# Seven half products in place of eight in a feed-forward's first product

## The chip, the cores and the metric

The kernel runs on one core of one Trainium2 chip, as one program. The metric is the device time of one execution in microseconds (us); the times shown are medians of several runs. A core has TensorE (PE, matrix products), VectorE (DVE), ScalarE (ACT), GpSimd (POOL) and SyncE (SP, whose queue issues most DMAs). Each engine works through its own instructions in order; semaphores join them.

## The reference

What is computed is a trunk of two layers over 256 tokens of width 1024. A layer is feed-forward, attention (three kinds, merged by gates), a second feed-forward and a gated embedding. The part that the change touches:

```
def rms_norm(x, g):
    y = x * rsqrt(mean(x * x, axis=-1) + 1e-6)
    return y * g

def swiglu(x, wi, wo):                  # wi 1024 x 5632, wo 2816 x 1024
    gate, up = split(x @ wi, 2, axis=-1)
    return (silu(gate) * up) @ wo

for i in range(2):
    h = h + 0.5 * swiglu(rms_norm(h, norm_g[i, 0]), ffn1_wi[i], ffn1_wo[i])
    ...                                 # attention, added to h
    h = h + 0.5 * swiglu(rms_norm(h, norm_g[i, 2]), ffn2_wi[i], ffn2_wo[i])
    h = h + sigmoid(rms_norm(h, norm_g[i, 3]) @ w_ple_gate[i]) * (p[i] @ w_ple[i])
return rms_norm(h, final_norm)
```

## The kernel before

**Tiles.** The 256 tokens are two tiles t0 and t1 of 128. Tokens are the stationary operand of a matmul (128 x 128: 128 of the 1024 inputs by 128 tokens), weights the moving one (128 x 512). A product over 1024 inputs is eight such k blocks.

**Three matmuls per product.** Each fp32 number is split in a high part, which the matrix unit's fp32r type holds, and a low rest. `mul3` (L234 to L237) adds xh·wh, xh·wl and xl·wh into one PSUM bank. `split` makes the two parts: ACT copies the high part (L228), DVE subtracts it from the source (`sub`, L223).

**Weights.** They are streamed in pieces of 512 KB (128 x 1024 fp32, two k blocks of one 512-wide column group). `load` issues a DMA on SP into a `raw` buffer (L278; four of them), and splits it into `wh` and `wl` (six of each). `queue` lists the pieces in the order of use; `fetch` runs two pieces ahead of the product (`AHEAD`).

**A feed-forward.** `ffn` is the same for all four. Its first product has 11 column groups (`FG`), each with 256 gate and 256 up columns. `product` walks the eight k blocks of a group for both tiles, t1 some blocks behind t0 (`SKEW`): 11 x 8 x 2 x 3 = 528 matmuls into the banks `ff`. When a group is done, `gated` takes silu of the gate half on ACT (L474) and multiplies by the up half on DVE (L475). Two groups fill a 128 x 512 tile, which `turn_by_dma` transposes: DVE copies the low and high 16-bit halves apart (`cut`, L442), two DMAs on SP transpose them (`flip`, L443), and later DVE joins them (`whole`, L448), whereupon they are split into gT. The second product (`fo`) takes gT as tokens.

**Tokens.** `Norm.turn` transposes half a tile (4 x 128) on PE into a bank `nt`; `Norm.turned` scales it by the norm's gain, per 128 columns one ACT copy (L336) and one DVE subtraction (L340), into nT. The first norm takes its tokens ready transposed from memory (`xt`).

**Space and order.** The pool `blk` has six buffers of 1 MB, shared by nT, xt and the attention's tiles; `stage` has four of 128 x 512. PSUM has two banks each of `mm` and `s`, three of `tp`, one of `y`. Which instruction stands where in each engine's row is set when the program is built, by a scheduler that works from priorities (`tc.high_priority`) and the tiles' uses; buffers come free in the order of use, and the instruction that takes one waits for its last reader.

Of the kernel before, what the change touches and what calls it, by code (L numbers as in the profile page):

```python
# [10 lines left out]
F32 = mybir.dt.float32  # L11
F32R = mybir.dt.float32r
# [174 lines left out]
def trunk(ctx: ExitStack, tc: tile.TileContext, a: dict, out: bass.AP, index: list):  # L187
# [21 lines left out]
    def tp_bank(name):  # L209
        return bank("tp", 3, name)  # L210
# [8 lines left out]
    def stage(name="stage"):  # L219
        return base.tile([128, 512], F32, tag="stage", bufs=4, name=name)  # L220

    def sub(o, x, y):
        nc.vector.tensor_tensor(o, x, y, op=ALU.subtract)  # L223

    def split(hi, lo, src, scale=None):

        if scale is None:
            nc.scalar.activation(hi, src, AF.Copy)  # L228
# [5 lines left out]
    def mul3(ps, xh, xl, wh, wl, start, stop):  # L234
        nc.tensor.matmul(ps, xh, wh, start=start, stop=False)  # L235
        nc.tensor.matmul(ps, xh, wl, start=False, stop=False)  # L236
        nc.tensor.matmul(ps, xl, wh, start=False, stop=stop)  # L237

    def transposes(ps, srcs):
        w = srcs[0].shape[-1]  # L240
# [7 lines left out]
    class Weights:  # L248


        def __init__(self, width, pieces, per):
            self.width, self.per = width, per
            self.tiles = [None] * len(pieces)
            self.at = [len(queue) + j for j in range(len(pieces))]
            queue.extend((self, j, src, n) for j, (src, n) in enumerate(pieces))
# [9 lines left out]

    def fetch(n):
        while fetched[0] < min(n, len(queue)):
            w, j, src, width = queue[fetched[0]]
            w.tiles[j] = load(src, width, 2 if fetched[0] < 2 else 1)
            fetched[0] += 1  # L270

    def load(src, n, parts=1):
        raw = base.tile([128, SUB], F32, tag="raw", bufs=RAWS, name="raw")
        hi = base.tile([128, SUB], F32R, tag="wh", bufs=WBUFS, name="wh")
        lo = base.tile([128, SUB], F32R, tag="wl", bufs=WBUFS, name="wl")
        for p in range(parts):
            s = slice(p * n // parts, (p + 1) * n // parts)
            nc.sync.dma_start(raw[:, s], src[:, s])  # L278
# [7 lines left out]
        where[i, n] = (pos, c)  # L286
        pos += c

    def streamed(i, name, width):
        p, c = where[i, name]  # L290
        return Weights(width, [(a["wst"][p + j], SUB) for j in range(c)], SUB // width)

    def last_product(lhs, nk, done, name, w):

# [10 lines left out]
    def product(lhs, nk, done, name, w, skew=SKEW):  # L305

        def run():
            ps = [None] * NT
            for step in range(nk + skew):
                for t, k in ((0, step), (1, step - skew)):  # L310
                    if 0 <= k < nk:
                        wh, wl = w(k)
                        if k == 0:
                            ps[t] = product_bank(f"{name}{t}")
                        xh, xl = lhs(t, k)
                        mul3(ps[t][:, :w.width], xh, xl, wh, wl, k == 0, k == nk - 1)
                        if k == nk - 1:
                            with tc.high_priority(offset=150):
                                done(t, ps[t])
                        flow.tick()  # L320
        return run


    class Norm:
        def __init__(self, row):
            self.row = row
            self.stat = [stats[:, row, t, :] for t in range(NT)]
            self.T = [None] * NT

        def turned(self, t, k, src, pin=False):  # L330

            if self.T[t] is None:
                self.T[t] = blk("nT")
            T, n = self.T[t], src.shape[-1] // 128
            for m in range(n):
                ins = nc.scalar.activation(T[:, 0, k + m, :], src[:, 128 * m:128 * m + 128], AF.Copy, scale=ngt[:, self.row, k + m:k + m + 1])  # L336
                if pin:
                    tc.keep_in_program_order(ins)
            for m in range(n):
                nc.vector.scalar_tensor_tensor(T[:, 1, k + m, :], src[:, 128 * m:128 * m + 128], ngt[:, self.row, k + m:k + m + 1],  # L340
                                               T[:, 0, k + m, :].bitcast(F32), op0=ALU.mult, op1=ALU.subtract)

        def turn(self, t, c):
            ps = tp_bank("nt")
# [87 lines left out]
    def halves(x):  # L432

        return x.bitcast(U16).rearrange("p (n w) -> p n w", w=2)

    def turn_by_dma(pool, src, m):


        cut = stage("cut").bitcast(U16).rearrange("p (w n) -> p w n", w=2)
        flip = pool.tile([128, 2, 4, 128], U16, tag="flip", bufs=3, name="flip")  # L440
        for w in range(2):
            nc.vector.tensor_copy(cut[:, w, :128 * m], halves(src)[:, :128 * m, w])  # L442
            nc.sync.dma_start(flip[:, w, :m], cut[:, w, :128 * m], transpose=True)  # L443

        def collect():
            whole = stage("whole")
            for w in range(2):
                tc.keep_in_program_order(nc.vector.tensor_copy(  # L448
                    halves(whole)[:, :128 * m, w], flip[:, w, :m].rearrange("p a b -> p (a b)")))
            return whole[:, :128 * m].rearrange("p (k q) -> p k q", q=128)  # L450
        return collect

    def ffn(i, n, norm, after, aside=None):
        pool = None
        gT, held, pending = [None] * NT, {}, {}
# [7 lines left out]
        def collect(t):  # L463
            if t in pending:
                first, m, whole = pending.pop(t)
                split(gT[t][:, 0, first:first + m, :], gT[t][:, 1, first:first + m, :], whole())

        def gated(f):
            def done(t, ps):
                collect(t)  # L470
                if f % 2 == 0:
                    held[t] = pool.tile([128, 512], F32, tag="gated", bufs=4, name="gated")
                act = pool.tile([128, 256], F32, tag="act", bufs=3, name="act")
                nc.scalar.activation(act, ps[:, :256], AF.Silu, scale=norm.r(t))  # L474
                nc.vector.tensor_tensor(held[t][:, 256 * (f % 2):256 * (f % 2) + 256], act, ps[:, 256:], op=ALU.mult)  # L475
                if f % 2 or f == FG - 1:
                    first, m = f - f % 2, 2 * (f % 2 + 1)
                    pending[t] = 2 * first, m, turn_by_dma(pool, held[t], m)
            return done

        def gathered(t, k):
            if k == 8:
                collect(t)
            return gT[t][:, 0, k, :], gT[t][:, 1, k, :]

        steps = []

        def beside():
            if not steps:
                steps.append(aside(pool))  # L490
            next(steps[0])

        yield begin
        for f in range(FG):
            yield product(norm.lhs, NK, gated(f), "ff", streamed(i, f"{n}{f}", 512), 2 if aside and f == 0 else SKEW)
            if aside and f in (4, 5, 8):
                yield beside
# [618 lines left out]
    def setup(pool):  # L1116
# [16 lines left out]
        tb_ps = tp_bank("tb")  # L1133
        nc.tensor.matmul(tb_ps[:NB, :REV], relb, onehot, start=True, stop=True)
        tb = pool.tile([NB, REV], F32, name="tb")
# [6 lines left out]
        lprod = pool.tile([128, 4, 64], F32, name="lprod")  # L1142
# [104 lines left out]
```

## Time and profile before

| what | value |
|---|---|
| median of three runs | 1339.92 us (1339.54 to 1340.08) |
| profiled execution, span | 1338.5 us, TensorE clock 0.999 |
| PE busy | 1322.5 us (99%), 6414 matmuls |
| PE weight loads | 1091.2 us (82%), beside the matmuls |
| DVE busy | 948.1 us (71%) |
| ACT busy | 778.7 us (58%) |
| DMA | 257.14 MB, mean 192 GB/s |

The profiled execution is one run with the profiler on; its span goes from the first instruction to the last, and the runs' times also hold what lies around it. Busy shares are of the span. PE is busy in nearly all of it, and matmuls overlap one another, so that their durations add to more than their spacing. The four feed-forwards' first products stand at about 5 to 131, 461 to 581, 671 to 792 and 1120 to 1241 us of the span.

### The profile page before, as it was taken

What the parts mean: (1) busy time and instruction counts of PE and PEld (TensorE: products, weight loads), DVE (VectorE), ACT (ScalarE), POOL (GpSimd) and SP (SyncE); (2) the same over time, 40 slices, a digit from 0 to 9 for tenths busy, and PEclk for the clock granted to TensorE, in tenths of its full rate; (3) what the DMA queues carried; (4) which work ended last, traced back from release to release, by engine and by line L of the source; (5) the groups of instructions that cost most, each with busy time, mean ns of one, the idle gap of its engine ahead of it and who ended that gap; (6) DMA issues with size and microseconds to landing.
All of it is one profiled execution on the core that took longest, in us unless ns stands there. A gap on an engine that the chain in (4) does not pass through costs nothing.

```text
span 1338.5 us, 18237 instructions
## 1 busy us (share of the span) xinstructions
PE 1322.5 (99%) x6414; PEld 1091.2 (82%) x6414; DVE 948.1 (71%) x1791; ACT 778.7 (58%) x1378; POOL 18.6 (1%) x36
## 2 busy tenths in 40 slices
PE   9999999999999999999999999999999999999997
PEld 7778888888887788888888888888888878888886
DVE  6677566768978767665767765677688886767665
ACT  7555455668756655544655545566695656555454
POOL 0000000000000000000000000000000000000000
PEclk9999999999999999999999999999999999999999
DMA  8887665345652577675567875744556435877662
GB/s 298 220 260 221 210 200 202 115 159 192 221 162 90 187 206 220 209 217 180 197 191 222 216 213 188 245 152 152 180 162 220 144 101 180 238 221 214 191 208 79
DMA packets 121993, 257.14 MB, mean 192 GB/s; under 512 B 56944, under 2 KB 62500, under 8 KB 121902
## 3 DMA queue, kind: packets, MB, share of 16 engines
q1 hardware_dynamic: 121150, 254.34, 61.2%
q0 software_dynamic: 320, 1.08, 0.3%
q8 instruction: 50, 0.82, 0.3%
q10 hardware_dynamic: 432, 0.56, 0.1%
q14 instruction: 41, 0.34, 0.1%
HBM read 243.33 MB, written 1.08 MB: 183 GB/s over the span
## 4 chain that ended last, share of the span: by engine, by line
PE 91%; DMA 3%; DVE 3%; ACT 1%; issue 1%; SPq 0%; POOLq 0%; POOL 0%; DVEq 0%; ACTq 0%
PE ff L236 11%; PE ff L235 11%; PE ff L237 11%; PE fo L235 6%; PE fo L236 6%; PE fo L237 6%; PE gate L235 3%; PE gate L237 3%; PE gate L236 3%; PE s L537 2%; PE A L236 2%; PE A L235 2%; PE A L237 2%; PE br L235 2%; PE br L236 2%; PE br L237 1%
## 5 line engine op out<-in xcount | busy, mean ns | idle before, releaser
L223 DVE TENSOR_TENSOR wl<-raw,wh 128x1024 fp32r<-128x1024 f32 (+1 forms) x448 | 539.1, 1213 | 160.6 <-ACT wh L228 154.7
L228 ACT ACTIVATE wh<-raw 128x1024 fp32r<-128x1024 f32 (+1 forms) x448 | 468.0, 1051 | 228.0 <-PE fo L237 85.0
L236 PE MATMUL ff<-wl,nT 128*128 128x512 f32 x704 | 273.4, 391 | 1.8 <-DVE wl L223 1.7
L237 PE MATMUL ff<-wh,nT 128*128 128x512 f32 x704 | 272.6, 390 | 0.0
L235 PE MATMUL ff<-wh,nT 128*128 128x512 f32 x704 | 270.4, 391 | 0.5 <-ACT nT L336 0.5
L236 PEld LDWEIGHTS ff<-wl,nT 128*128 128x128 f32 x704 | 132.3, 188 | 31.2 <-DVE wl L223 4.0
L235 PEld LDWEIGHTS ff<-wh,nT 128*128 128x128 f32 x704 | 132.2, 188 | 29.8 <-ACT wh L228 1.1
L237 PEld LDWEIGHTS ff<-wh,nT 128*128 128x128 f32 x704 | 132.3, 188 | 27.4
L236 PE MATMUL fo<-wl,gT 128*128 128x512 f32 x352 | 134.2, 392 | 0.0
L237 PE MATMUL fo<-wh,gT 128*128 128x512 f32 x352 | 133.7, 389 | 0.0
L235 PE MATMUL fo<-wh,gT 128*128 128x512 f32 x352 | 132.5, 389 | 0.0
L474 ACT ACTIVATE act<-ff,stats 128x256 f32<-128x256 f32 x88 | 41.4, 471 | 85.3 <-PE ff L237 85.1
L475 DVE TENSOR_TENSOR gated<-act,ff 128x256 f32<-128x256 f32 x88 | 36.6, 417 | 65.3 <-ACT act L474 65.2
L235 PEld LDWEIGHTS fo<-wh,gT 128*128 128x128 f32 x352 | 66.1, 188 | 13.9
L237 PEld LDWEIGHTS fo<-wh,gT 128*128 128x128 f32 x352 | 66.1, 188 | 13.4
L236 PEld LDWEIGHTS fo<-wl,gT 128*128 128x128 f32 x352 | 66.1, 188 | 13.3
L235 PE MATMUL gate<-wh,nT 128*128 128x512 f32 x192 | 76.8, 400 | 0.0
L236 PE MATMUL gate<-wl,nT 128*128 128x512 f32 x192 | 76.2, 397 | 0.0
L237 PE MATMUL gate<-wh,nT 128*128 128x512 f32 x192 | 75.9, 395 | 0.0
L228 ACT ACTIVATE gT<-whole 128x512 fp32r<-128x512 f32 (+1 forms) x48 | 28.4, 591 | 64.5 <-DVE whole L448 64.3
L548 ACT ACTIVATE p<-p,st 128x128 f32<-128x128 f32 (+1 forms) x128 | 56.7, 446 | 6.3 <-DVE st L546 6.1
L448 DVE COPY whole<-flip 128x512 uint16<-128x512 uint16 (+1 forms) x96 | 38.1, 434 | 12.8 <-DMA flip<-cut 12.1
(301 smaller groups left out, 1994.5 us busy)
## 6 DMA issues: line engine op xcount, KB each, us to landing
raw<-in_wst SPq DMA_DIRECT2D x438, 512.0 KB, 4.4
band<-table SPq DMA_DIRECT2D x10, 512.0 KB, 4.7
raw<-in_wbv SPq DMA_DIRECT2D x4, 420.0 KB, 3.1
flip<-cut SPq DMA_TRANSPOSE x96, 4.0
xt<-in_xt SPq DMA_DIRECT2D x4, 256.0 KB, 5.8
raw<-in_wst SPq DMA_DIRECT2D x4, 256.0 KB, 4.5
h<-in_x SPq DMA_DIRECT2D x2, 512.0 KB, 7.8
band<-table POOLq DMA_DIRECT2D x2, 512.0 KB, 5.5
```

What stands on the lines that cost most here:

```text
L223: nc.vector.tensor_tensor(o, x, y, op=ALU.subtract)
L228: nc.scalar.activation(hi, src, AF.Copy)
L235: nc.tensor.matmul(ps, xh, wh, start=start, stop=False)
L236: nc.tensor.matmul(ps, xh, wl, start=False, stop=False)
L237: nc.tensor.matmul(ps, xl, wh, start=False, stop=stop)
L448: tc.keep_in_program_order(nc.vector.tensor_copy(halves(whole)[:, :128 * m, w], flip[:, w, :m].rearrange("p a b -> p (a b)")))
L474: nc.scalar.activation(act, ps[:, :256], AF.Silu, scale=norm.r(t))
L475: nc.vector.tensor_tensor(held[t][:, 256 * (f % 2):256 * (f % 2) + 256], act, ps[:, 256:], op=ALU.mult)
L537: nc.tensor.matmul(o, q[r, x, qb[m], t * 128:(t + 1) * 128], kk, start=x + y == 0, stop=x == 1)
L548: nc.scalar.activation(p[j], p[j], AF.Exp, bias=st[:, j:j + 1], scale=-1.0, accum_out=st[:, n + j:n + j + 1])
```

## The change

Two pairs of column groups in each feed-forward, (2, 3) and (8, 9), are computed by another formula (`Seven`, `seven`, `combine`). A pair is a product of a 2 x 2 array of token blocks (two tiles by two halves of the inputs) with a 2 x 2 array of weight blocks (two halves of the inputs by two column groups). It takes eight half products of 12 matmuls; the new code takes seven products of sums of blocks, the banks p1, p5, p6 and p7 holding them. The first product then has 504 matmuls, not 528.

- Token sums: four per feed-forward (`combine`, one DVE operation each, L565, and a split into `xs`). They need all scaled tokens kept (`xg`, in a `blk` buffer).
- Weight sums: `Seven.make` loads the blocks into x and y (two areas in `blk` buffers) and into raw buffers (L301), and subtracts them on DVE in place (`minus`, L223 with outputs x, y or raw, 128 x 1024): eight per pair. Each of the seven blocks is then split like plain weights, two pieces each.
- Results: the bank p1 is copied to v by ACT (L617), and five additions per pair on DVE join the banks.
- Order: `lines` cuts the product into 42 lines of 12 matmuls: four of the first plain group, then 14 lines of sevens mixed among 24 plain ones. Seven-lines come in the order 11, t1, t2, t3, 22, 21, t4.
- `turn_by_dma` parts the halves with one ACT operation of 1024 16-bit elements, transposes them by one DMA of eight 128-blocks, and joins them with one DVE copy. It is collected three lines later.
- `Norm.turned` scales 512 columns at once on DVE (L409), copies the high part on ACT (L410) and subtracts on DVE.
- The set-up's table product goes to an `mm` bank, and two small tiles share others' space.

```diff
+    class Seven:
...
+        order = ("11", "t1", "t2", "t3", "22", "21", "t4")
...
+        def __init__(self, i, fa, fb, x, y):
+            self.src = {"11": (fa, 0), "12": (fb, 0), "22": (fb, 2), "21": (fa, 2)}
...
+        def minus(self, n, x, y):
+            self.raw[n] = self.raw[y]
+            for j in range(2):
+                sub(self.raw[y][j], self.raw[x][j], self.raw[y][j])
...
+        def make(self, n):
+            if n == "11":
+                self.fill("11", self.x())
+            elif n == "t1":
+                self.fill("12", self.y())
+                self.minus("t1", "12", "11")
+            elif n == "t2":
+                self.fill("22")
+                self.minus("t2", "22", "t1")
+            elif n == "t3":
+                self.minus("t3", "22", "12")
+            elif n == "21":
+                self.fill("21")
+            elif n == "t4":
+                self.minus("t4", "21", "t2")
...
         def turned(self, t, k, src, pin=False):
...
-            for m in range(n):
-                ins = nc.scalar.activation(T[:, 0, k + m, :], src[:, 128 * m:128 * m + 128], AF.Copy, scale=ngt[:, self.row, k + m:k + m + 1])
...
+            ins = [nc.vector.tensor_tensor(scaled, src.rearrange("p (m q) -> p m q", q=128), g[:, :, None].to_broadcast([128, n, 128]), op=ALU.mult),
+                   nc.scalar.activation(T[:, 0, k:k + n, :], scaled, AF.Copy)]
...
+            sub(T[:, 1, k:k + n, :], scaled, T[:, 0, k:k + n, :].bitcast(F32))
...
     def turn_by_dma(pool, src, m):
...
-        for w in range(2):
-            nc.vector.tensor_copy(cut[:, w, :128 * m], halves(src)[:, :128 * m, w])
-            nc.sync.dma_start(flip[:, w, :m], cut[:, w, :128 * m], transpose=True)
...
+        nc.scalar.activation(cut.rearrange("p (w n) -> p w n", w=2), halves(src)[:, :128 * m].rearrange("p n w -> p w n"), AF.Copy)
+        nc.sync.dma_start(flip, cut, transpose=True)
...
+        def seven(fa, fb, w):
...
+            times(p1, lambda k: norm.lhs(0, k), "11", True)
+            with tc.high_priority(offset=150):
+                nc.scalar.activation(v, p1, AF.Copy)
+            yield
+            times(p5, sums[1], "t1", True)
+            yield
+            times(p6, sums[2], "t2", True)
+            with tc.high_priority(offset=150):
+                nc.vector.tensor_tensor(v, v, p6, op=ALU.add)
+            yield
+            times(p7, sums[3], "t3", True)
+            with tc.high_priority(offset=150):
+                x = plus("w", v, p7)
+                gated(fb, 1, plus("c22", x, p5))
+            yield
+            times(p5, sums[4], "22", False)
+            with tc.high_priority(offset=150):
+                gated(fb, 0, plus("c12", v, p5))
+            yield
+            times(p1, lambda k: norm.lhs(0, 4 + k), "21", False)
+            with tc.high_priority(offset=150):
+                gated(fa, 0, p1)
+            yield
+            times(p7, lambda k: norm.lhs(1, 4 + k), "t4", False)
+            with tc.high_priority(offset=150):
+                gated(fa, 1, plus("c21", v, p7))
+            yield
...
-        for f in range(FG):
-            yield product(norm.lhs, NK, gated(f), "ff", streamed(i, f"{n}{f}", 512), 2 if aside and f == 0 else SKEW)
...
+            kinds, m = [0] * 4, 0
+            for j in range(24):
+                kinds.append(0)
+                m += 14
+                if m >= 24:
+                    m -= 24
+                    kinds.append(1)
+            kinds[4:] = kinds[:3:-1]
+            groups = [iter([0, 1, 4, 5, 6, 7, 10]), iter([(2, 3), (8, 9)])]
...
+            if aside and at in (19, 24, 34):
+                beside()
```

The engines' rows change most where a feed-forward begins. In the rows below, the name ahead of `<-` is the output, those behind it the inputs; x and y are the areas of weights, xs the token sums' parts.

DVE's row at the start of the second feed-forward of the first layer, before:

```order
L377 SCALAR_TENSOR_TENSOR h<-wo_4475,h 128x512
L340 SCALAR_TENSOR_TENSOR nT<-nt,ngt,nT 128x128 x4
L223 TENSOR_TENSOR wl<-raw,wh 128x1024
L355 SCALAR_TENSOR_TENSOR stats<-stats 128x1
L340 SCALAR_TENSOR_TENSOR nT<-nt,ngt,nT 128x128 x4
L357 TENSOR_SCALAR stats<-stats 128x1
L358 TENSOR_SCALAR stats<-stats 128x1
L340 SCALAR_TENSOR_TENSOR nT<-nt,ngt,nT 128x128 x4
L223 TENSOR_TENSOR wl<-raw,wh 128x1024
L475 TENSOR_TENSOR gated<-act,ff_4533 128x256
L223 TENSOR_TENSOR wl<-raw,wh 128x1024 x2
L475 TENSOR_TENSOR gated<-act,ff_4580 128x256
```

and in the changed kernel, the rows up to the weights of its first two seven-lines:

```order
L565 TENSOR_TENSOR sum<-xg 128x512
L223 TENSOR_TENSOR xs<-sum,xs 128x512 x3
L548 TENSOR_TENSOR gated<-act,ff_4518 128x256
L223 TENSOR_TENSOR wl<-x,wh 128x1024
L548 TENSOR_TENSOR gated<-act,ff_4531 128x256
L223 TENSOR_TENSOR wl<-x,wh 128x1024
L223 TENSOR_TENSOR x<-y,x 128x1024
L223 TENSOR_TENSOR wl<-raw,wh 128x1024
L223 TENSOR_TENSOR x<-y,x 128x1024
L223 TENSOR_TENSOR y<-raw,y 128x1024
L223 TENSOR_TENSOR wl<-x,wh 128x1024 x2
L223 TENSOR_TENSOR y<-raw,y 128x1024
```

The token sums and their splits now stand ahead of the first gated half, and the weight differences stand between the splits.

ACT's row at the same place, before:

```order
L350 ACTIVATE sq,stats<-h 128x512
L336 ACTIVATE nT<-nt,ngt 128x128 x8
L228 ACTIVATE wh<-raw 128x1024
L474 ACT_TABLE_LOAD
L474 ACTIVATE act<-ff_4533,stats 128x256
L228 ACTIVATE wh<-raw 128x1024 x2
L474 ACTIVATE act<-ff_4580,stats 128x256
```

and in the changed kernel:

```order
L410 ACTIVATE nT<-xg 128x512 x2
L228 ACTIVATE xs<-sum 128x512 x4
L546 ACT_TABLE_LOAD
L546 ACTIVATE act<-ff_4518,stats 128x256
L228 ACTIVATE wh<-x 128x1024
L546 ACTIVATE act<-ff_4531,stats 128x256
L228 ACTIVATE wh<-x 128x1024
L228 ACTIVATE wh<-raw 128x1024
L228 ACTIVATE wh<-x 128x1024
L617 ACTIVATE v<-p_4617 128x512
```

The high parts of the token sums moved ahead of the table load, and the first of x's high parts stands behind the first silu.

SP's row at the kernel's start, before:

```order
L278 DMA raw<-in_wst 128x1024
L1215 DMA h<-in_x 128x1024 x2
L1219 DMA ident<-in_ident 128x128
L278 DMA raw<-in_wst 128x1024 x12
L443 DMA_TRANSPOSE flip<-cut 128x4x128 x2
```

and in the changed kernel:

```order
L1403 DMA h<-in_x 128x1024 x2
L1407 DMA ident<-in_ident 128x128
L341 DMA raw<-in_wst 128x1024 x3
L301 DMA raw<-in_wst 128x1024
L301 DMA x<-in_wst 128x1024 x2
L301 DMA y<-in_wst 128x1024 x2
L301 DMA raw<-in_wst 128x1024
L341 DMA raw<-in_wst 128x1024 x4
L301 DMA y<-in_wst 128x1024 x2
L341 DMA raw<-in_wst 128x1024
L301 DMA raw<-in_wst 128x1024
L516 DMA_TRANSPOSE flip<-cut 128x8x128
```

The loads of x and y took places among the raw pieces; the first transpose stands behind more loads.

More of the change, by code (lines that the diff above doesn't have):

```diff
@@ L232, in split, with mul3 @@
             nc.vector.scalar_tensor_tensor(lo, src, scale, hi.bitcast(F32), op0=ALU.mult, op1=ALU.subtract)
[L234 to L237, printed above, removed]
+    def mul3(ps, xh, xl, wh, wl, start, stop, **kw):
+        nc.tensor.matmul(ps, xh, wh, start=start, stop=False, **kw)
+        nc.tensor.matmul(ps, xh, wl, start=False, stop=False, **kw)
+        nc.tensor.matmul(ps, xl, wh, start=False, stop=stop, **kw)
     def transposes(ps, srcs):
@@ L248, in trunk, with __init__, push @@
     class Weights:
[L251 to L255, printed above, removed]
+        def __init__(self, width, pieces, per, push=True):
+            self.width, self.per, self.pieces = width, per, pieces
+            self.tiles, self.at = [None] * len(pieces), [None] * len(pieces)
+            if push:
+                for j in range(len(pieces)):
+                    self.push(j)
+        def push(self, j):
+            self.at[j] = len(queue)
+            queue.append(lambda: self.tiles.__setitem__(j, load(*self.pieces[j], 2 if self.at[j] < 2 else 1)))
         def __call__(self, k):
@@ L328, in __init__, with keep @@
             self.T = [None] * NT
+            self.kept = None
+        def keep(self):
+            self.kept = base.tile([128, NT, NK, 128], F32, tag="blk", bufs=6, name="xg")
         def turned(self, t, k, src, pin=False):
@@ L334, in turned @@
             T, n = self.T[t], src.shape[-1] // 128
-            for m in range(n):
[L336 to L341, printed above, removed]
+            g = ngt[:, self.row, k:k + n]
+            if self.row % 2 == 0 and self.row < 4 * DEPTH:
+                if self.kept is None:
+                    self.keep()
+                scaled = self.kept[:, t, k:k + n, :]
+            else:
+                scaled = stage("scaled")[:, :128 * n].rearrange("p (m q) -> p m q", q=128)
+            ins = [nc.vector.tensor_tensor(scaled, src.rearrange("p (m q) -> p m q", q=128), g[:, :, None].to_broadcast([128, n, 128]), op=ALU.mult),
+                   nc.scalar.activation(T[:, 0, k:k + n, :], scaled, AF.Copy)]
+            if pin:
+                for x in ins:
+                    tc.keep_in_program_order(x)
+            sub(T[:, 1, k:k + n, :], scaled, T[:, 0, k:k + n, :].bitcast(F32))
         def turn(self, t, c):
@@ L454, in ffn @@
         pool = None
-        gT, held, pending = [None] * NT, {}, {}
+        gT, held, pending, now = [None] * NT, {}, [[] for _ in range(NT)], [0]
+        sums, spare = {}, []
         def begin():
@@ L461, in begin, with collect, gated @@
                 gT[t] = pool.tile([128, 2, NF, 128], F32R, name=f"gT{t}")
-        def collect(t):
-            if t in pending:
-                first, m, whole = pending.pop(t)
+        def collect(t, all=False):
+            while pending[t] and (all or pending[t][0][0] <= now[0]):
+                _, first, m, whole = pending[t].pop(0)
                 split(gT[t][:, 0, first:first + m, :], gT[t][:, 1, first:first + m, :], whole())
[L468 to L479, printed above, removed]
+        def gated(f, t, x):
+            first = f - f % 2
+            if (first, t) not in held:
+                held[first, t] = [pool.tile([128, 512], F32, tag="gated", bufs=4, name="gated"), 0]
+            act = pool.tile([128, 256], F32, tag="act", bufs=3, name="act")
+            nc.scalar.activation(act, x[:, :256], AF.Silu, scale=norm.r(t))
+            to = held[first, t]
+            nc.vector.tensor_tensor(to[0][:, 256 * (f % 2):256 * (f % 2) + 256], act, x[:, 256:], op=ALU.mult)
+            to[1] += 1
+            if to[1] == 2 or f == FG - 1:
+                pending[t].append((now[0] + 3, 2 * first, 2 * to[1], turn_by_dma(pool, to[0], 2 * to[1])))
@@ new lines, in lines @@
+        def lines():
+            kinds, m = [0] * 4, 0
[7 more added lines that the diff above has]
+            groups = [iter([0, 1, 4, 5, 6, 7, 10]), iter([(2, 3), (8, 9)])]
+            at, line, w = [0, 0], [None] * 2, [None] * 2
+            for kind in kinds:
+                if at[kind] == 0:
+                    g = next(groups[kind])
+                    w[kind] = Seven(i, f"{n}{g[0]}", f"{n}{g[1]}", area(0), area(1)) if kind else streamed(i, f"{n}{g}", 512, False)
+                    line[kind] = seven(*g, w[1]) if kind else plain(g, w[0])
+                w[kind].push(at[kind])
+                at[kind] = (at[kind] + 1) % (7 if kind else 4)
+                yield line[kind]
@@ L491, in beside, with products @@
             next(steps[0])
+        steps, ahead = [], list(lines())
+        def products():
+            make = combine()
+            for at, line in enumerate(ahead):
+                now[0] += 1
+                for t in range(NT):
+                    with tc.high_priority(offset=150):
+                        collect(t)
+                if at < 4:
+                    next(make)
+                next(line)
+                if aside and at in (19, 24, 34):
+                    beside()
         yield begin
-        for f in range(FG):
-            yield product(norm.lhs, NK, gated(f), "ff", streamed(i, f"{n}{f}", 512), 2 if aside and f == 0 else SKEW)
-            if aside and f in (4, 5, 8):
-                yield beside
+        yield products
         for c in range(2):
```

97 lines of the change are left out of this document (84 added, 13 removed).

## The prediction

> **What bounds the kernel now.** I read the page's busy shares first, then its chain, then the four stretches in which a feed-forward's first product runs.
>
> ```profile
> PE 1322.5 (99%) x6414; PEld 1091.2 (82%) x6414; DVE 948.1 (71%) x1791; ACT 778.7 (58%) x1378; POOL 18.6 (1%) x36
> PE 91%; DMA 3%; DVE 3%; ACT 1%; issue 1%; SPq 0%; POOLq 0%; POOL 0%; DVEq 0%; ACTq 0%
> core 0: us, PE busy (x) PEld busy (x) DVE busy (x) ACT busy (x) POOL busy (x), PEclk, DMA share, GB/s
> 5.00:131.00 126.00, 123.71 (x531) 99.06 (x531) 93.37 (x156) 74.14 (x107) 3.47 (x5) 1.00 0.84 253
> 460.70:581.20 120.50, 120.50 (x536) 99.76 (x536) 86.38 (x136) 66.16 (x93) 1.12 (x2) 1.00 0.73 211
> 671.30:791.80 120.50, 120.50 (x537) 99.77 (x537) 85.87 (x131) 63.50 (x87) 0.55 (x1) 1.00 0.73 213
> 1120.20:1240.70 120.50, 120.50 (x537) 99.71 (x537) 86.25 (x136) 66.19 (x93) 1.12 (x2) 1.00 0.74 212
> ```
>
> PE is busy all the time and 91% of the chain. In each of the four stages it is busy from end to end at full clock, with one exception at the kernel's start. But DVE is already busy for 86 of 120.5 us there, and the weights flow at over 210 GB/s. So matmuls are the bound, and DVE is the engine with the least room behind them. The waits say the same: matrices wait for nothing in these stages, and the weight queue waits for DVE.
>
> ```profile
> PE ff L236 <- DVE wl L223: 1.7, 1, 1.7
> SPq L278 <- DVE wl L223: 529.5, 248, 8.6
> 468.33 0.39 PE L236 MATMUL ff<-wl,nT 128*128 128x512 f32 x1
> 468.56 0.39 PE L237 MATMUL ff<-wh,nT 128*128 128x512 f32 x1
> 468.78 0.39 PE L235 MATMUL ff<-wh,nT 128*128 128x512 f32 x1
> 469.01 0.39 PE L236 MATMUL ff<-wl,nT 128*128 128x512 f32 x1
> ```
>
> The timeline rows guard against a trap. A matmul lasts 0.39 us, but the starts are 0.227 us apart: the matmuls overlap, and the price of one is the spacing. 528 of them at 0.2267 make 119.7 us, which is the stage.
>
> **What is removed.** Each feed-forward loses 24 of 528 matmuls, 5.44 us; the four lose 96, 21.8 us. That is certain only while PE never waits. A stage then has 114.3 us of matmuls.
>
> **What is added, nearly all on DVE.** Its durations overlap in the same way, so I price by the distance to the next start.
>
> ```profile
> L223 DVE TENSOR_TENSOR wl<-raw,wh 128x1024 fp32r<-128x1024 f32 x438 | 531.0, 1221 | 158.3 <-ACT wh L228 152.4
> L228 ACT ACTIVATE wh<-raw 128x1024 fp32r<-128x1024 f32 x438 | 460.6, 1058 | 226.0 <-PE fo L237 85.0 <-PE ff L237 38.0 <-issue 31.1
> 20.59 0.42 DVE L475 TENSOR_TENSOR gated<-act,ff 128x256 f32<-128x256 f32 x1
> 20.92 2.36 DVE L223 TENSOR_TENSOR wl<-raw,wh 128x1024 fp32r<-128x1024 f32 x2
> 506.80 0.76 DVE L442 COPY cut<-gated 128x512 uint16<-128x512 uint16 x2
> 507.48 1.22 DVE L223 TENSOR_TENSOR wl<-raw,wh 128x1024 fp32r<-128x1024 f32 x1
> 508.61 0.80 DVE L448 COPY whole<-flip 128x512 uint16<-128x512 uint16 x2
> 514.51 0.69 DVE L223 TENSOR_TENSOR gT<-whole,gT 128x512 fp32r<-128x512 f32 x1
> 515.11 2.36 DVE L223 TENSOR_TENSOR wl<-raw,wh 128x1024 fp32r<-128x1024 f32 x2
> L223 DVE TENSOR_TENSOR gT<-whole,gT 128x512 fp32r<-128x512 f32 x40 | 27.5, 688 | 12.6 <-ACT gT L228 12.6
> L970 DVE SCALAR_TENSOR_TENSOR th<-th,br 128x512 f32<-128x512 f32 x16 | 10.9, 682 | 3.2 <-PE br L237 3.2
> ```
>
> A 1024-wide subtraction costs 1.135 us (507.48 to 508.61), a 512-wide one 0.60 (514.51 to 515.11), a gated half 0.33 (20.59 to 20.92), one cut copy 0.34 (two from 506.80 to 507.48), one whole copy about 0.37 (its duration less the overlap of the others). The ledger of DVE for one first product:
> - before: 44 wl x 1.135 = 49.9, 22 gated x 0.33 = 7.3, 20 cut x 0.34 and the short last ones = 7.6, whole 7.8, gT 6.7: 79.3 us of PE's 119.7. With the tokens' own work at the stage's start this is the 86 us of the windows.
> - after: 56 wl x 1.135 = 63.6, because 14 seven-lines of two pieces each replace 16 pieces of plain weights; 16 weight differences of the same shape, 18.2; ten additions out of PSUM, 512 wide, 6.0; the token sums and their splits, 8 x 0.6 = 4.8; gated 7.3, whole 7.8, gT 6.7: 114.4 us of PE's 114.3.
>
> So DVE goes from two thirds to full. The single whole copy of 1024 has no row; two old ones make 0.69 (bounds 0.35 and 0.92), and I keep 0.69, since the element count is the same. An addition takes one operand from PSUM, as L970's row does: 682 ns against 688 for gT's subtraction, so it costs 0.60 as well.
>
> The Trainium skill ("VectorE: DVE Perf Modes", section "Why `tensor_tensor` can't do 2×_2P or 4×") says that an elementwise operation with two tensors cannot use the fastest modes, which single-source copies can. The rows agree (1024 fp32 by two operands 1.135 us, a 512 u16 copy 0.34), and it speaks against this change: what is taken off DVE is the cheap kind, what is put on it the dear kind.
>
> On ACT, 12 more wh are 12.7 us at 1.06, the cuts move there as ten operations of 1024 u16 (about 1.06 each by the wh row, 0.6 to 1.2), v and the sums' high halves are six of about 0.6. Less the eight single scaled copies, ACT comes to about 82 to 90 of 114 us. It is no bound.
>
> **Where DVE's fullness is paid.** An average at 100% leaves nothing to catch up with, so what counts is how late DVE is when the first seven-line begins. After four plain lines (48 matmuls, 10.9 us, plus 0.7 for transposes among them) p1 wants x's first split.
>
> ```profile
> 460.77 0.40 PE L235 MATMUL ff<-wh,nT 128*128 128x512 f32 x1
> 462.97 0.68 DVE L377 SCALAR_TENSOR_TENSOR h<-wo,h 128x512 f32<-128x512 f32 x1
> 471.75 1.28 ACT L474 ACT_TABLE_LOAD   x1 [2.79 <-PE ff L237]
> 473.04 0.47 ACT L474 ACTIVATE act<-ff,stats 128x256 f32<-128x256 f32 x1
> raw<-in_wst SPq DMA_DIRECT2D x438, 512.0 KB, 4.4
> ```
>
> *Second feed-forwards (two of them, behind wo), t = 0 at 460.77.* The last residual ends 2.9 us in (462.97 and 0.68), and there the last transposes stand in the changed kernel's order too. Scaling and four sums follow in DVE's row: scaled at 4.5, sums done 8.7. Only then may y (which takes the scaled tokens' buffer) be loaded; at 4.4 us a piece, two behind one another, it is there at 13.3 to 15. ACT meanwhile stands at its table load, which waits for the first group's last matmul as in the row at 471.75 (then 9.8 us in, now as well): 11.1 loaded, 11.5 act, 12.5 x's high half, 13.75 its low half from DVE; wanted at 11.85. That is 1.9 us late. From there to the second piece of the next plain group DVE's row holds nine 1024-wide operations and a gated half, 10.55 us, while PE has 37 matmuls, 8.4: 2.1 more. Together 4.1 us (with rounding) per stage. y's landing gives nearly the same: 14.2, then four operations and the first wl of t1 at 19.9 against 17.5.
>
> *First feed-forward of the second layer.* The last transposes wait for the gate's residual and stand 5.9 us in by the order, not 2.9.
>
> ```profile
> 671.13 0.39 PE L237 MATMUL pg<-wh,nT 128*128 128x512 f32 x1
> 681.10 1.14 ACT L336 ACTIVATE nT<-nt,ngt 128x128 fp32r<-128x128 f32 x4 [2.30 <-PE nt L243]
> ```
>
> In the trace they came later still, since the second tile's tokens were only copied 9.8 us after the stage's start (681.10). With 5.9, y lands at about 16.5 and t1's first wl is done at 22.2 against 17.5: 4.7 late, and 0.9 more until the plain piece: 5.6 us.
>
> *First feed-forward of all.* It starts with the DMAs full.
>
> ```profile
> 10.00:20.00 10.00, 9.90 (x43) 7.55 (x42) 8.15 (x23) 9.86 (x23) 1.11 (x2) 1.00 0.99 392
> 14.34 1.22 DVE L223 TENSOR_TENSOR wl<-raw,wh 128x1024 fp32r<-128x1024 f32 x1
> 5.07 0.69 PE L235 MATMUL ff<-wh,nT 128*128 128x512 f32 x1
> ```
>
> x stands on SP behind four more raw pieces, the last of which needs the buffer that the subtraction at 14.34 frees at 15.6. Until x's end 7.4 MB must have come; 2.5 in the first 10 us, the rest at 392 GB/s: 22.5. p1's low half is done 23.8, wanted at 17.5: 6.3 late. y comes another 1 MB later (25.2), and DVE's row adds 1.7: 8.0 us.
>
> *Rest of the stages.* After the start DVE is level with PE to within 3 us by the order, and every raw piece that it frees late delays a load; half the weight queue's waits are for wl already. I put 1.5 us a stage for such waits (0 if the two stay level, 4 if each of four transposes and whole copies costs one piece), 6 in all.
>
> **Everything else at nothing.** Scaling 512 wide takes DVE 1.2 us for 1.03 per half tile and ACT 0.5 for 1.0, and the second half is needed over 6 us later. One transpose of 8 x 128 in place of two leaves the same bytes on SP and half the issues. Collecting three lines later (8 us) is covered by the second product, which reads the early groups first. The set-up steps stay where they were in time. Together -2 to +2.
>
> **The sum.** -21.8 + 8.0 + 5.6 + 4.1 + 4.1 + 6.0 = +6.0 us. The profiled execution spans 1338.5, and the median of the runs is 1339.9, 1.4 more for what lies around it. 1339.9 + 6.0 = 1346.
>
> **Rivals.**
> *Faster, chance 0.31.* The starts are hidden better: ACT's rows are short, x lands earlier, and DVE's additions are cheap. For: PE today never waits in these stages, and buffers of six pieces carry 8 us. Against: DVE's ledger. The rival ends below the 0.2% line if the four stages wait under 19.1 us in all (4.8 each, where I have 27.8). With half my waits, 13.9, and no lag later: 1339.9 - 21.8 + 10.9 = 1329.
> *No change that can be measured, chance 0.17.* A measurement of this kernel tells about 0.2% (2.7 us) from nothing. Waits between 19.1 and 24.5 us; for example the second feed-forwards at 3 and the rest as above: 1340.
> *DVE bounds the whole stage, chance 0.09.* If the whole copies cost their upper bound (0.92), DVE has 116.7 us, and each of the last three stages lasts this plus the start in which DVE waits, 6 to 8 us: 123 to 125 against 120.5, with 6 more in the first in all 14 to 20 us: 1354 to 1360.
> The Trainium skill ("TensorE: Matmul & The Clock Gate", section "Part 1: The HAM clock gate") adds that an idle window of about 3.4 us halves PE's clock until it is busy for another. No run here shows it (the longest wait was 1.7 us, the clock 1.00); by it the waits of 4 to 6 us at the starts would cost up to 2 us each on top and lean to this rival.
> *My forecast, slower by 3 to 12 us, chance 0.43.*
>
> **How the numbers follow.** The likeliest case gives 1346, its own range 1343 to 1352. The range 1328 to 1361 takes in the rival of half waits and the full DVE. Faster 0.31, same 0.17, slower 0.43 + 0.09 = 0.52.
>
> **What would show it.** 96 fewer matmuls of 512; PE waits at the first seven-line for wh or wl out of x, 2 us and more, in all four stages; the last three stages at about 120 to 122 us and the first near 130; DVE over 95% busy in them. I am wrong if PE stays busy there (the stages then last 115), or if DVE shows idle time while PE waits for data.

## The result and the profile after

The changed kernel takes 1357.5 us (1357.4 to 1357.7), the kernel before 1339.7 beside it: a ratio of 1.0134, 95% interval 1.0122 to 1.0147. It is 17.8 us slower. The forecast was 6 us slower, 1346, with 1343 to 1352 as its own case and 1328 to 1361 as the whole range.

The page's busy shares, the chain and the four stretches of the first products (columns as before), of the changed kernel:

```profile
PE 1318.0 (97%) x6318; PEld 1076.0 (79%) x6318; DVE 1077.2 (79%) x1769; ACT 859.9 (63%) x1403; POOL 24.7 (2%) x36
PE 67%; DVE 17%; DMA 7%; issue 4%; ACT 4%; SPq 0%; POOL 0%; ACTq 0%; DVEq 0%; POOLq 0%
5.10:139.40 134.30, 124.71 (x507) 97.04 (x507) 119.20 (x153) 90.66 (x117) 5.05 (x5) 0.99 0.74 229
469.10:591.10 122.00, 117.89 (x514) 94.64 (x513) 110.86 (x134) 84.41 (x105) 1.11 (x2) 1.00 0.66 199
681.10:807.50 126.40, 120.06 (x514) 97.32 (x513) 111.97 (x130) 82.69 (x102) 0.65 (x2) 0.97 0.65 196
1135.90:1258.10 122.20, 118.19 (x513) 94.71 (x513) 112.40 (x134) 84.17 (x106) 1.12 (x2) 1.00 0.68 201
```

The 96 matmuls are gone (6318 of 6414). But PE's share of the chain fell from 91 to 67%, and DVE's rose from 3 to 17%. The four stages last 134.1, 121.9, 126.2 and 122.0 us from their first matmul to their last, against 125.8, 120.4, 120.4 and 120.4 before: 17.0 us more, nearly the whole difference. DVE is busy 111 to 119 us in each, 89 to 92% of its stage. The other stages kept their lengths (the second products 61.0 us each, before and after).

What PE waited for, in us in all, times, and the longest, of the changed kernel:

```profile
PE p L235 <- ACT wh L228: 10.0, 9, 2.5
PE p L236 <- DVE wl L223: 5.5, 5, 2.5
PE ff L236 <- DVE wl L223: 4.7, 8, 1.1
PE ff L235 <- ACT wh L228: 1.7, 5, 0.5
```

Before, there was one such wait of 1.7 us. Here `p` stands for the banks of the seven-lines. They wait for the two parts of their weights. (This view counts only the time from the end of one matmul to the start of the next. The sums below count all that a start is late, and so are larger.)

To see where in a stage the time is lost, I summed over all matmuls of the stages what each start is later than 0.2267 us behind the one before:

| lost in the four stages, us | first 10 us | 10 to 40 us | after 40 us |
|---|---|---|---|
| before | 2.6, 0.3, 0.2, 0.3 | 0.4, 0, 0, 0 | 2.6, 0, 0, 0 |
| changed | 5.3, 0.2, 0.2, 0.1 | 5.0, 4.4, 5.9, 4.1 | 9.0, 2.5, 5.3, 2.9 |

96 matmuls fewer save 21.8. Beyond the first 10 us 39.1 are lost in place of 3.0, and the kernel's first 10 us cost 2.7 more: +17.0.

A part of the loss is the clock. The matmuls at the first seven-line of the kernel, on PE's timeline, and four short stretches with the granted clock as third figure from the end:

```profile
21.08 0.39 PE L237 MATMUL ff<-wh,nT 128*128 128x512 f32 x1
23.31 0.50 PE L235 MATMUL p<-wh,nT 128*128 128x512 f32 x1 [1.84 <-ACT wh L228]
24.57 0.79 PE L236 MATMUL p<-wl,nT 128*128 128x512 f32 x1 [0.76 <-DVE wl L223]
25.16 0.63 PE L237 MATMUL p<-wh,nT 128*128 128x512 f32 x1
25.59 0.63 PE L235 MATMUL p<-wh,nT 128*128 128x512 f32 x1
```

```profile
24.00:28.00 4.00, 3.43 (x8) 2.73 (x9) 4.00 (x5) 2.21 (x3) 0.00 (x0) 0.57 0.14 54
696.00:700.00 4.00, 4.00 (x11) 3.21 (x12) 4.00 (x4) 1.63 (x2) 0.00 (x0) 0.61 0.13 52
780.00:784.00 4.00, 2.20 (x6) 1.77 (x7) 4.00 (x6) 1.86 (x3) 0.00 (x0) 0.77 0.79 259
784.00:788.00 4.00, 4.00 (x15) 3.20 (x15) 4.00 (x5) 1.64 (x2) 0.00 (x0) 0.80 0.74 255
```

From 25.16 on the starts are 0.43 us apart, not 0.227, for some 3 us. This happened three times in the four stages behind their first 10 us and cost 1.6, 1.6 and 1.7 us, 4.9 in all.

The 2.7 us of the kernel's first 10 us are mostly of the same kind. In the changed kernel's profile the starts are 0.43 us apart until 13.86 us (the views give no lower clock there), while the prediction's row of before has 43 matmuls from 10 to 20 us, 0.23 apart:

```profile
13.44 0.63 PE L235 MATMUL ff<-wh,nT 128*128 128x512 f32 x1
13.86 0.55 PE L236 MATMUL ff<-wl,nT 128*128 128x512 f32 x1
```

It isn't shown that the change brought this about: two kernels of the next section that begin alike lost 2.9 and 4.2 us there.

### The profile page after: what moved, and what is told of

Read it like the earlier page. It is cut to its first block, busy times and chain, and to the rows that moved or that the text cites. A ratio compares the mean times of both kernels' runs of the same rounds, so it can differ in the third digit from the quotient of the medians.

```text
span 1355.8 us, 17986 instructions
## 1 busy us (share of the span) xinstructions
PE 1318.0 (97%) x6318; PEld 1076.0 (79%) x6318; DVE 1077.2 (79%) x1769; ACT 859.9 (63%) x1403; POOL 24.7 (2%) x36
## 4 chain that ended last, share of the span: by engine, by line
PE 67%; DVE 17%; DMA 7%; issue 4%; ACT 4%; SPq 0%; POOL 0%; ACTq 0%; DVEq 0%; POOLq 0%
DVE wl L223 9%; PE fo L237 6%; PE fo L235 6%; PE fo L236 6%; DMA raw<-in_wst 4%; PE gate L235 3%; PE gate L237 3%; PE gate L236 3%; PE ff L236 2%; PE ff L237 2%; PE ff L235 2%; ACT wh L228 2%; PE s L725 2%; PE A L237 2%; PE A L235 2%
## 5 line engine op out<-in xcount | busy, mean ns | idle before, releaser
L223 DVE TENSOR_TENSOR wl<-raw,wh 128x1024 fp32r<-128x1024 f32 (+2 forms) x416 | 499.5, 1211 | 122.0 <-ACT wh L228 116.8
L228 ACT ACTIVATE wh<-raw 128x1024 fp32r<-128x1024 f32 (+2 forms) x416 | 432.4, 1048 | 209.2 <-DMA raw<-in_wst 88.8
L236 PE MATMUL ff<-wl,nT 128*128 128x512 f32 x448 | 178.0, 398 | 4.9 <-DVE wl L223 4.7
L237 PE MATMUL ff<-wh,nT 128*128 128x512 f32 x448 | 176.3, 395 | 0.2 <-DVE nT L223 0.2
L235 PE MATMUL ff<-wh,nT 128*128 128x512 f32 x448 | 167.2, 399 | 2.1 <-ACT wh L228 1.7
L236 PEld LDWEIGHTS ff<-wl,nT 128*128 128x128 f32 x448 | 85.3, 190 | 28.1 <-DVE wl L223 10.8
L235 PEld LDWEIGHTS ff<-wh,nT 128*128 128x128 f32 x448 | 85.3, 191 | 23.7 <-ACT wh L228 4.7
L228 ACT ACTIVATE wh<-x 128x1024 fp32r<-128x1024 f32 x64 | 66.8, 1056 | 58.5 <-DVE x L223 45.7
L237 PEld LDWEIGHTS ff<-wh,nT 128*128 128x128 f32 x448 | 85.4, 191 | 18.3 <-DVE nT L223 0.8
L223 DVE TENSOR_TENSOR wl<-x,wh 128x1024 fp32r<-128x1024 f32 x64 | 77.3, 1220 | 4.9 <-ACT wh L228 4.1
L236 PE MATMUL p<-wl,xs 128*128 128x512 f32 x128 | 50.4, 394 | 3.7 <-DVE wl L223 2.5
L235 PE MATMUL p<-wh,xs 128*128 128x512 f32 x128 | 50.2, 392 | 2.0 <-ACT wh L228 2.0
```

The costliest lines, as they stand in the source:

```text
L235: nc.tensor.matmul(ps, xh, wh, start=start, stop=False, **kw)
L236: nc.tensor.matmul(ps, xh, wl, start=False, stop=False, **kw)
L237: nc.tensor.matmul(ps, xl, wh, start=False, stop=stop, **kw)
```

## The experiments

Theory: the loss is DVE's, in two parts, the weights of the first seven-lines coming late at a stage's start, and DVE being full afterwards. Rivals: the other edits (cut on ACT, one transpose, wide scaling, later collecting) cost it; ACT's order costs it; the place of the sevens, not DVE's work, costs it.

**The other edits alone.** All groups plain:

```diff
-            kinds, m = [0] * 4, 0
...
+            kinds = [0] * 44
+            groups = [iter(range(FG)), iter([])]
```

> All eleven column groups are computed the plain way, in lines of 12 matmuls; the wide token scaling, the kept tokens, the cut on ACT, the single transpose and the later collecting stay. My theory (the seven-lines make DVE full, and the rest is free): 1337 to 1343 us, the four stages within 1 us of before's 125.8 and 120.4. Rival (the other edits cost a part of the 17.8 us): 1346 us or more, with waits of matrices on whole, gT or nT.

1339.4 us, a ratio of 0.9993 (0.9983 to 1.0002). Its first and second stages:

```profile
5.00:129.00 124.00, 122.51 (x533) 99.31 (x533) 85.94 (x117) 81.18 (x108) 3.36 (x5) 1.00 0.84 264
458.40:578.90 120.50, 120.50 (x536) 99.71 (x536) 78.94 (x98) 73.80 (x93) 1.12 (x2) 1.00 0.71 217
```

PE waits for nothing in the last three stages and for 0.6 us at most in the first, and DVE has even 7 us less to do than before (78.9 against 86.4); the cut that moved to ACT is 20 copies at 0.34, 6.8 us. The first stage is 123.35 us long, 2.5 less than before. So the other edits cost nothing, and the loss belongs to the sevens.

**One pair, early or late.** One pair (2, 3) from the fifth line on, or one pair (8, 9) after 24 plain lines:

```diff
+            kinds, m = [0] * 24, 0
+            for j in range(12):
...
+                m += 7
...
+            groups = [iter([0, 1, 2, 3, 4, 5, 6, 7, 10]), iter([(8, 9)])]
```

> One pair a feed-forward, (2, 3), its seven-lines mixed with plain ones from the fifth line on as now, then 20 plain lines; 48 matmuls fewer than before, 10.9 us. If the loss sits at the stage's beginning (the first seven-lines wait for token sums, x and y; in the changed kernel the losses up to 25 us after the stages' starts are about 5 us each): 1339.7 - 10.9 + 19 = 1348 us. If it sits in DVE's fullness throughout, it halves with the pairs: 1339.7 + 9 = 1349 for equal halves of the 17.8, and the losses lie spread over the lines; the stage lengths alone do not part the two, the places of the waits do.

> One pair a feed-forward, (8, 9), after 24 plain lines; again 48 matmuls fewer. If the loss sits at the stage's beginning: 1339.7 - 10.9 = 1329 to 1332 us. If it is DVE's fullness wherever the sevens stand: like one_early, 1345 to 1350.

Early: 1350.5 us, 1.0083 (1.0066 to 1.01), near the 1348 expected. Late: 1337.6, 0.998 (0.9971 to 0.999), between the two cases that I had named. The early pair lost 19.2 us between 10 and 40 us of its stages and 2.1 later: the whole loss of the starts is there with one pair, the later loss isn't. The late pair's last three stages were 117.7, 118.1 and 117.7 us. Two of them are 2.7 shorter than before, all that 12 matmuls are worth:

```profile
466.70:584.50 117.80, 117.80 (x525) 97.50 (x524) 94.91 (x115) 78.27 (x98) 1.12 (x2) 1.00 0.70 210
```

Seven-lines among plain ones as densely as in the changed kernel thus cost nothing in two of these stages and 0.4 us in the third, where they begin late and are few. The late pair lost 9.3 us in the first stage, 5.8 of them in one wait, and so missed the 1329 to 1332.

**A later start for both pairs.** Eight plain lines first, not four:

```diff
-            kinds, m = [0] * 4, 0
-            for j in range(24):
+            kinds, m = [0] * 8, 0
+            for j in range(20):
```

> Both pairs, but the first seven-line stands behind eight plain lines in place of four, so the token sums, x and y have 10.9 us more to arrive. If the losses at the stages' starts (19 us in the changed kernel) come from that arrival, they go: 1357.5 - 19 = 1338 us, or up to 1344 since the 14 seven-lines now stand among 20 plain ones and DVE has less time for them. Rival (DVE's sum of work decides, wherever the sevens stand): 1354 us or more.

1339.8 us, 0.999 (0.998 to 1.0), as expected. Between 10 and 40 us 4.1 are lost in place of 19.4. Afterwards it is 20.5 against 19.7, 12.4 of it in the first stage: the second part of the loss stays. The start's loss is one of arrival. In the changed kernel ACT's timeline of the first layer's second feed-forward reads (with DVE's first low part of x last):

```profile
478.12 1.18 ACT L228 ACTIVATE xs<-sum 128x512 fp32r<-128x512 f32 x2 [0.63 <-DVE sum L565]
479.31 1.28 ACT L546 ACT_TABLE_LOAD   x1
480.61 0.47 ACT L546 ACTIVATE act<-ff,stats 128x256 f32<-128x256 f32 x1
480.98 1.04 ACT L228 ACTIVATE wh<-x 128x1024 fp32r<-128x1024 f32 x1
482.06 1.23 DVE L223 TENSOR_TENSOR wl<-x,wh 128x1024 fp32r<-128x1024 f32 x1 [0.52 <-ACT wh L228]
```

and with eight plain lines x's high part stands ahead of the table load:

```profile
478.63 1.13 ACT L228 ACTIVATE xs<-sum 128x512 fp32r<-128x512 f32 x2
479.67 1.05 ACT L228 ACTIVATE wh<-x 128x1024 fp32r<-128x1024 f32 x1
481.36 1.06 ACT L228 ACTIVATE wh<-x 128x1024 fp32r<-128x1024 f32 x1 [0.64 <-PE ff L237]
482.76 1.28 ACT L546 ACT_TABLE_LOAD   x1 [0.34 <-PE ff L237]
```

**DVE's work, taken away and added.** Four runs with the sevens as in the changed kernel: without the weight differences; the joining copy on ACT; the cut on DVE; the differences on POOL.

```diff
# no_diffs
-            for j in range(2):
-                sub(self.raw[y][j], self.raw[x][j], self.raw[y][j])
# whole_act
-            tc.keep_in_program_order(nc.vector.tensor_copy(
+            tc.keep_in_program_order(nc.scalar.activation(
...
# cut_dve
-        nc.scalar.activation(cut.rearrange("p (w n) -> p w n", w=2), halves(src)[:, :128 * m].rearrange("p n w -> p w n"), AF.Copy)
+        for q in range(2):
+            nc.vector.tensor_copy(cut.rearrange("p (w n) -> p w n", w=2)[:, q], halves(src)[:, :128 * m, q])
# pool_diffs
-                sub(self.raw[y][j], self.raw[x][j], self.raw[y][j])
+                nc.gpsimd.tensor_tensor(self.raw[y][j], self.raw[x][j], self.raw[y][j], op=ALU.subtract)
```

> The changed kernel without the 16 weight differences of each feed-forward (the seven-lines multiply the blocks as they are loaded, so this part of the computation is left out): DVE does 18.2 us less a stage, and t1 doesn't wait for y. If DVE's work is what makes the weights late, 1328 to 1338 us: the four first waits for x remain (about 8 us) and those beside the set-up. Rival (ACT's order, raw buffers held by the sevens, or the transposes delay the weights): 1345 us or more.

> The changed kernel with the joining copy (whole) on ACT in place of DVE: DVE does about 7 us less a stage, ACT about 10 more (84 of 122 us now). Taking 18.2 us a stage off DVE gave 25.8 us in all; in proportion this gives 10: 1347 us (1343 to 1351). Rival (the order on ACT is what delays the high parts): 1357 or more.

> The changed kernel with the halves parted by two copies on DVE, as before the change, in place of one on ACT: DVE does 6.8 us more a stage, ACT 10 less. If DVE's sum decides: 10 us slower in proportion, 1367 us (1362 to 1375). Rival (the cuts that stand in a row on ACT ahead of x's high part are what delays the late seven-lines): 1350 to 1357 us.

> Both pairs as in the changed kernel, but the 16 weight differences of a feed-forward run on POOL, which is idle there. My theory: DVE's ledger falls from 114 to 96 us a stage; if POOL takes less than about 4 us for one, most waits after the start vanish: 1335 to 1345 us, with DVE's busy time near 93 us a stage. Rival (POOL is too slow, or slows DVE): the sevens wait for POOL and the time is 1360 us or more.

| kernel | DVE's work a stage, by the prices of the prediction, us | time, us | ratio and interval | lost 10 to 40 us | lost after 40 us |
|---|---|---|---|---|---|
| without differences | 18.2 less | 1331.7 | 0.9922 (0.9907 to 0.9938) | 13.3 | 0.2 |
| joining copy on ACT | about 7 less | 1351.1 | 1.0079 (1.0062 to 1.0096) | 20.2 | 13.3 |
| changed kernel | 0 | 1357.5 | 1.0134 (1.0122 to 1.0147) | 19.4 | 19.7 |
| cut on DVE | 6.8 more | 1368.8 | 1.0211 (1.0192 to 1.0229) | 18.2 | 32.9 |

The first and the last row came out in the ranges expected, the joining copy at the upper edge of its range. The later loss follows DVE's work at every step, though ACT's moved the other way in the second and fourth rows. So it is not ACT's load that sets it here. Nor is the clock the whole of it: the joining copy on ACT left 13.3 us with no slow stretch after 40 us. The starts' loss follows DVE only in part: a third of it went with the differences, which also spared the second seven-line its wait for y, and the other two runs hardly changed it. Without differences all four stages are free of waits after 40 us, the first with its set-up too. The second stage there and with the cut on DVE:

```profile
459.60:578.70 119.10, 117.33 (x514) 96.44 (x513) 95.68 (x120) 84.20 (x105) 1.11 (x2) 0.99 0.69 205
467.70:595.10 127.40, 119.95 (x513) 95.72 (x512) 119.93 (x153) 75.49 (x96) 1.12 (x2) 0.99 0.63 195
```

How DVE's lateness reaches PE is seen at the longest late wait of the changed kernel, in the third stage (timelines of SP, DVE, ACT and PE, and one line of the weight queue's waits):

```profile
776.13 3.37 SPq L301 DMA_DIRECT2D raw<-in_wst  x2
773.74 2.36 DVE L223 TENSOR_TENSOR wl<-raw,wh 128x1024 fp32r<-128x1024 f32 x2 [0.52 <-ACT wh L228]
777.91 2.37 DVE L223 TENSOR_TENSOR wl<-raw,wh 128x1024 fp32r<-128x1024 f32 x2
778.74 1.06 ACT L228 ACTIVATE wh<-raw 128x1024 fp32r<-128x1024 f32 x1 [0.95 <-DMA raw<-in_wst]
780.69 1.06 ACT L228 ACTIVATE wh<-raw 128x1024 fp32r<-128x1024 f32 x1 [0.37 <-DMA raw<-in_wst]
781.80 0.50 PE L235 MATMUL p<-wh,nT 128*128 128x512 f32 x1 [2.55 <-ACT wh L228]
SPq L341 <- DVE wl L223: 626.5, 273, 8.6
```

DVE is busy without a gap from 773.74 on. A raw buffer comes free when its low part is subtracted. The first of SP's two loads began at 776.13, behind the pair of subtractions that ended at 776.10. ACT waited for its landing until 780.69, and PE for ACT's high part until 781.80. SP's second load waited in the same way for the subtraction that began at 777.91; in all, SP's plain weight loads waited 626.5 us for DVE's low parts, before 529.5. A late DVE so delays its own next weights, and then waits itself for ACT's high part, as the 0.52 us at 773.74 show. PE's wait of 2.55 us was followed by a stretch at the low clock that cost 1.7 us.

POOL is a miss, as the rival had it: 1416.1 us, 1.0569 (1.0553 to 1.0584). One difference took it 2.4 to 2.7 times DVE's 1.22 us, and it slowed DVE beside it. POOL's line, and DVE's low parts of x with POOL at work and in the changed kernel:

```profile
L307 POOL TENSOR_TENSOR x<-raw,x 128x1024 f32<-128x1024 f32 x32 | 99.8, 3134 | 152.2 <-DMA raw<-in_wst 149.9 <-DVE wl L223 2.3
L223 DVE TENSOR_TENSOR wl<-x,wh 128x1024 fp32r<-128x1024 f32 x64 | 128.0, 2010 | 7.7 <-ACT wh L228 7.0
L223 DVE TENSOR_TENSOR wl<-x,wh 128x1024 fp32r<-128x1024 f32 x64 | 77.3, 1220 | 4.9 <-ACT wh L228 4.1
```

The Trainium skill ("GPSIMD Engine Reference", section "1. Specifications") says that POOL shares its SBUF interfaces with DVE and that DVE instructions with two SBUF inputs suffer. The 2010 against 1220 ns agree. They are a mean of two kinds: 32 of DVE's weight subtractions ran for nine tenths of their time or more beside POOL's and took 3.2 us in the mean, as long as POOL's, and those with POOL idle took 1.2. Two beside POOL, each in turn, on the timelines of POOL and DVE:

```profile
499.01 6.70 POOL L307 TENSOR_TENSOR y<-raw,y 128x1024 f32<-128x1024 f32 x2
496.71 6.77 DVE L223 TENSOR_TENSOR wl<-x,wh 128x1024 fp32r<-128x1024 f32 x2
```

**The first stage, and better versions.** The late pair with the set-up's steps ahead of it; the late pair with a plain first stage; both pairs behind eight plain lines with a plain first stage, and the same with the joining copy on ACT.

```diff
# late_setup
-                if aside and at in (19, 24, 34):
+                if aside and at in (7, 12, 20):
# late3, start8x3, s8x3_wact
+            if aside:
+                kinds, groups = [0] * 44, [iter(range(FG)), iter([])]
```

> One pair a feed-forward, (8, 9), after 24 plain lines, in all four; the set-up's three steps stand behind lines 7, 12 and 20 of the first feed-forward, ahead of the sevens, in place of 19, 24 and 34. If the single wait of 5.8 us that the late pair had there comes from the set-up (a table load on ACT ahead of the silus, then transposes and joins late), it goes: 1337.6 - 6 = 1331 us or less. Rival (it is the sevens' DVE work behind a DMA-bound start): no change, 1336 to 1339, or slower as the set-up's loads meet the start's.

> The kernel's first feed-forward plain; in the other three one pair, (8, 9), after 24 plain lines. 36 matmuls fewer than before. If the one long wait of the late pair in the first feed-forward belongs to the set-up that runs beside it, the other three gain all of their 12 matmuls: 1339.7 - 8.2 = 1331.5, with the first stage as without pairs down to 1329. Rival (that wait is the sevens' own and chance): 1335 or more.

> The kernel's first feed-forward plain; in the other three both pairs, the first seven-line behind eight plain lines. The stages of the run with that start, 118.1, 120.2 and 116.6 us, and a plain first one of 123.3 in place of 132.3 give 1339.8 - 9 = 1331 us, no better than one late pair in the three, since DVE's fullness takes what the second pair saves.

> As the run with the plain first feed-forward and both pairs behind eight plain lines in the other three, with the joining copy on ACT. DVE has 7 us less to do a stage, and the three stages come near their matmuls, 115 to 116.5 us: 1323 to 1328 us, the best version. Rival (ACT, at 84 + 10 of 117 us, makes silus and high parts late): 1331 us or more.

Set-up moved: 1333.8 us, 0.9942 (0.9926 to 0.9958), a little more than expected. Its first stage lost 3.3 us after 40 us in place of 9.3: most of that loss was the meeting of the set-up and the sevens. Late pair in three stages: 1330.9, 0.992 (0.9902 to 0.9938), as expected and the best of all. Each of its three stages is 117.7 us:

```profile
458.40:576.20 117.80, 117.80 (x525) 97.51 (x524) 96.13 (x117) 77.20 (x98) 1.11 (x2) 1.00 0.68 208
```

Both pairs from the ninth line on, in three stages: 1333.7, 0.9955 (0.9939 to 0.997); the stages are 116.1, 120.6 and 117.3 us. The second pair's 2.7 us are given back. With the joining copy on ACT as well: 1336.8, 0.9975 (0.9965 to 0.9984), where I expected 1323 to 1328. Here the rival held: the later loss grew from 7.6 to 11.3 us, though DVE had less to do. The copy on ACT helped behind four plain lines and hurt behind eight. The trace shows a place where ACT is the late one. In each of the three stages two joining copies in a row, 2.6 us, stand on ACT straight ahead of a high part of x, and PE waits 1.0 us for it. In the last stage, on ACT's and PE's timelines:

```profile
1198.17 2.56 ACT L520 ACTIVATE whole<-flip 128x1024 uint16<-128x1024 uint16 x2
1200.60 1.03 ACT L228 ACTIVATE wh<-x 128x1024 fp32r<-128x1024 f32 x1
1201.68 0.50 PE L235 MATMUL p<-wh,xs 128*128 128x512 f32 x1 [0.96 <-ACT wh L228]
```

With the copy on DVE, PE's longest wait of each stage stood thereabouts too, 0.8, 1.6 and 1.5 us. So ACT's row only took the place of DVE's there. Which of ACT's instructions made the loss grow was not tried and stays open.

## Why the prediction was wrong

- *96 matmuls at 0.2267 us, 21.8 saved:* right. The late pair's stages are shorter by exactly 12 spacings.
- *DVE's ledger, 114.4 us a stage:* right in its prices (1.135 us from start to start for a 1024-wide subtraction, 0.60 for a 512-wide one), but not all of it falls in the stage. In the second stage 7 of 10 joining copies and 6 of 10 subtractions into gT ran by its end, some 4 us less, and DVE was busy 110.9 of 122.0 us with the tokens' own work in it. So the sign "DVE over 95% busy" did not come: it was 89 to 92%. Nor did DVE stand idle while PE waited late: behind the first 40 us of the last three stages there is no such moment.
- *The starts, 8.0 + 4.1 + 5.6 + 4.1 = 21.8:* 19.4 measured (5.0, 4.4, 5.9, 4.1). PE's two waits in the first seven-line were 2.6, 1.7, 2.3 and 1.3 us together, so my sign of 2 us and more came in two stages of four. For the second feed-forwards the reasons hold too: late x, then DVE's row. In the first layer's second feed-forward x's first low part ended 14.1 us after the stage's start (482.06 and 1.23, from 469.2), where I had 13.75. The first of all was over-sized: ACT took x's high part without a wait for its load, and PE lost 2.0 and 1.0 us to waits, and 1.6 to the clock. That the second layer's first feed-forward came near its 5.6 is luck: 1.6 of its 5.9 are the clock's, which the sum had at nothing.
- *Everything else at nothing:* right for the other edits (1339.4 us without pairs). Wrong for the set-up: its steps stood where they were, but now amid sevens. Moving them took 6 us from the loss of one late pair. How much of the changed kernel's 9.0 us in the first stage is theirs was not tried. The 3.0 us that the kernel before lost itself in its first stage, and the 2.7 of the kernel's start, were in no term either; they nearly cancel.
- *The rest of the stages, 1.5 us each, 6.0 in all:* this is the step that failed. It was 9.0, 2.5, 5.3 and 2.9, 19.7. I had set the whole stage's DVE work level with PE's and priced the unevenness at next to nothing. But with so little room DVE didn't make up its bursts: a late subtraction delays the load of a later piece, that load delays ACT, and some of DVE's free time then goes to waiting for ACT and the DMAs (7.3 us in the second stage after its first 40 us). This part hangs on DVE's work: 0.2 us are left without the differences, 32.9 with 6.8 us more work, and 1.7 of the 19.7 are the clock's after a wait of this kind.
- *The sum with what was measured:* -21.8 - 3.0 + 19.4 + 19.7 + 2.7 = +17.0, of the 17.8.
- *The rivals.* The time fell to the one that I gave 0.09, DVE as bound of the whole stage (1354 to 1360), though not by its price, a dear joining copy: the copy took 757 ns, little more than half of a 1024-wide subtraction's 1220. That the time fell there is partly luck, since DVE was not busy all the stage and 4.9 us are the clock's. But DVE as the limit of the later stage should have been my first case, since the ledger already said 114.4 of 114.3. The faster rival failed with the starts.
- *The clock.* By the Trainium skill ("TensorE: Matmul & The Clock Gate", section "Part 1: The HAM clock gate") an idle window of about 3.4 us lowers the clock until a busy one. The waits here that came ahead of a low clock were shorter than that: 2.55 us once, and twice a pair with one matmul between (1.84 and 0.76, 1.57 and 0.76). I let the clock only lean to a rival. The three stretches cost 4.9 us, beside a slowdown of 17.8.

## What to carry to other kernels

Where an engine off the path would be filled to nearly the bound's own time, price it as the bound: its bursts weren't made up here even at 91% busy, and it delayed the transfers whose buffers it frees. A saving on the bound was whole only where the helper engine kept room (12 matmuls for DVE at 96 of 118 us were worth all of 2.7 us a stage), so spend a trade only as far as that. And start such work late enough for its inputs to have arrived.

## What the runs showed of the hardware

- Waits of PE below 3 us were followed by a lower clock: behind 1.84 and 0.76 us with one matmul between them the spacings were 0.43 us for about 3 us (granted clock 0.57 from 24 to 28 us). A wait of 2.46 us that began at 98.8 us into the span had no such effect, so it depends on more than the length.
- POOL's subtraction of 128x1024 fp32 took 3.1 us. DVE's subtractions of that size that ran beside it nearly all their time took 3.2 us, in place of 1.2.
